# The weight sums of a decoder layer's first output product made ahead, during product pairs two to four

## Chip, cores, metric

The kernel runs on one core of one Trainium2 chip. The metric is the device time of one execution in microseconds (us); lower is better. Everything is float32 at the interface.

## What is computed

One layer of a hybrid decoder on 512 tokens of width 2048. The reference, cut to what matters:

```python
h = rms_norm(x, norm1_g)
proj = h @ w_in                                   # one combined projection
qa, ka, va, ra, ga, qb, kb, vb = split(proj)
out_a = gla_mixer(qa, ka, va, ra, log_g, onorm_g) # 4 heads of gated linear attention
out_b = dilated_mixer(norm(qb), norm(kb), vb)     # 8 heads of dilated attention
mix = concatenate([out_a, out_b])
x = x + mix @ w_out                               # the output product
x = x + (silu(h2 @ w_gate) * (h2 @ w_up)) @ w_down, with h2 = rms_norm(x, norm2_g)
```

The change concerns the left half of `mix @ w_out`: the weight columns 0 to 1023 of `w_out`, a matrix of 2048 x 2048.

## The kernel before

**Products in pairs.** Every large matrix product is done in pairs of weight blocks, two blocks of 512 columns each (`w1`, `w2`), by a scheme of the Strassen-Winograd kind: seven products of half size in place of eight. The object `Pair` (L236) stands for one pair. Its products come in the order P1, P5, P6, P3, P7, P2, P4 (L32), and each runs over `g`, the quarters of its inner dimension (four; three in two of the last pairs). One product at one `g` is called a **group** here; a pair of four quarters is 28 groups.

**The weights of a group.** A quarter of weights is a tile of 128 partitions x 1024 floats, 512 KB, two row blocks (j = 0, 1) of 128 rows x 512 columns. For each `g` there are four quarters, a, b, c, d: a and b are the upper rows of `w1` and `w2`, c and d the lower rows. P1, P3 and P2 use a quarter as it is (a, d, c). P5, P6, P7 and P4 use a difference: b - a, d - a, d - b, c - a, where the minuend of one may be the result of another, since `source` (L250) subtracts in place with one VectorE instruction (L256, 128x1024): P5 leaves b - a in a's tile, and so on. `load_quarter` (L219) loads a quarter through SyncE's DMA queue into the pool `wpool`, which has 12 buffers.

**The split.** Float32 matmuls are made of two rounded parts. `stream` (L318) runs through the groups of all pairs. For each it rounds the weights on ScalarE (`wh`, L331), subtracts that from the weights on VectorE (`wl`, L335, 128x1024), and issues 12 matmuls on TensorE (L372): eight with `wh`, four with `wl`. `wh` and `wl` have two buffers each. The work for group k + 1's parts and group k + 2's sum is written ahead of the matmuls of group k. After the eighth matmul of a group the pair's `step` is called (L378); it carries the background work: attention heads, normalisations, transposes and the building of later operands, so many units for each group (`rate`, `paced`). The operand's side is split in the same manner (ScalarE L174, VectorE L175, 128x512), and its sums are VectorE instructions too (L1256 to L1260 for the late operands).

**What sets the order.** The first pair is laid out by hand. After it, a scheduler orders the instructions of each engine by when it reckons their inputs ready, starting from the program's order; a buffer that is still in use holds its next user.

**The pairs in turn.** The first pair (by hand); va (pair two), query and key of the first four dilated heads (pair three), vb (pair four), the other queries and keys, the gates; then two output pairs (L1438, L1439), eleven pairs of the feed-forward part (FFN) and six of its down projection. In pairs two to four the attention units run in the background. In these, GpSimd does the small steps of `rsqrt_mean` (L158, L159): `so` for an output of a linear-attention head, which VectorE multiplies in at L938, and `ss` for the norms of query and key heads, which VectorE uses at L1086. GpSimd also copies decays (L864, L865) and clears a tile `PT` (L894). It issues no DMAs. The first output pair also builds parts of its own operand while it runs.

**The pool `rpool`** has four buffers of 256 KB: raw input during the first pair, parts of operands later, and one lane of a dilated head.

Of the kernel before, what the change touches and what calls it, by code (L numbers as in the profile page):

```python
# [10 lines left out]
F32 = mybir.dt.float32  # L11
# [3 lines left out]
ALU = mybir.AluOpType  # L15
# [3 lines left out]
P = 128  # L19
# [14 lines left out]
SINGLE = {"P1": "a", "P3": "d", "P2": "c"}  # L34
SUMS_OF = {"P5": "ba", "P6": "da", "P7": "db", "P4": "ca"}
# [72 lines left out]
def block_kernel(ctx: ExitStack, tc: tile.TileContext, ins, out):  # L108
    nc = tc.nc
    x, w_in, w_out, w_gate, w_up, w_down = (  # L110
        ins[n] for n in ("x", "w_in", "w_out", "w_gate", "w_up", "w_down")
    )
# [33 lines left out]
    load = nc.sync.dma_start  # L146
# [18 lines left out]
    class Operand:  # L165


        def __init__(self, groups):
            self.groups = groups
            self.t = {}  # L170
# [65 lines left out]
    class Pair:  # L236


        def __init__(self, op, rows, w1, w2, final, step, scale=None, before=None):
            self.op, self.rows, self.w1, self.w2 = op, rows, w1, w2  # L240
            self.final, self.step, self.scale, self.before = final, step, scale, before
            self.q, self.dst, self.held = {}, {}, {}

        def quarter(self, name, g):
# [5 lines left out]
        def source(self, prod, g):  # L250

            if prod in SINGLE:
                return self.quarter(SINGLE[prod], g)
            one, two = SUMS_OF[prod]
            src = self.quarter(two, g)
            nc.vector.tensor_tensor(src, self.quarter(one, g), src, op=ALU.subtract)  # L256
            return src
# [50 lines left out]
        def end(self, prod):  # L308
            src = self.dst[prod]
            if prod in ("P1", "P5", "P6"):  # L310
                self.held[prod] = self.seeds(src, int(prod == "P5"))
            elif prod == "P4":
                later(1, lambda: self.final(1, 0, None, src), hold=True)
            else:
                which = {"P3": "P6", "P7": "P5", "P2": "P1"}[prod]
                self.close(self.held[which], src, *CLOSES[prod])

    def stream(pairs):  # L318

# [65 lines left out]
    def soon(fn, groups=1):  # L385

        soonest.append([groups, fn])

    def run_soon():
        for d in list(soonest):  # L390
            d[0] -= 1
            if d[0] <= 0:
                soonest.remove(d)
                d[1]()
# [114 lines left out]
    def later(units, fn, hold=False):  # L509

        deferred.append([units, fn, hold])
# [20 lines left out]
    def finish(ready):  # L532

        tries = 0
        while not ready():
            tries += 1
            assert tries < 100
            run_soon()
            try:
                next(background[0])  # L540
            except StopIteration:
                background.pop(0)

    def paced(counts):
        counts = iter(counts)
        return lambda: step(next(counts, 1))

    def rate(*stretches):


        owed = [0.0]
        rates = iter([r for n, r in stretches for _ in range(n)])

        def go():
            owed[0] += next(rates, stretches[-1][1])
            n = owed[0] if owed[0] > 0.3 else 0
            owed[0] = min(owed[0] - (step(n) or 0.0), 1.0)

        return go
# [79 lines left out]
    row_scale = lambda half, m: rs1[:, 2 * half + m : 2 * half + m + 1]  # L639
# [464 lines left out]
    order = (2, 3, 0, 1)  # L1104

    def final_proj(n1, n2):
        def final(half, which, tiles, acc_):
            if tiles is None:
                tiles = emitted(acc_, lambda m: row_scale(half, m))
            name = (n1, n2)[which]  # L1110
            dst = proj[name]
            for m in range(2):
                r = half * 256 + m * P
                put = lambda r=r, m=m: store(dst[r : r + P, :], tiles[m])
                if name[:2] in ("qb", "kb"):
# [183 lines left out]
    opm = Operand(4)  # L1299
    pairs = []  # L1300

    def pair(*args, **kw):
        pairs.append(Pair(*args, **kw))

    pair(opx, rows_in, col(1536), col(1024), final_proj("va1", "va0"), rate((22, 1), (6, 0.6)),
         row_scale, before=lambda: background.extend([gates(), bias_tables()]))
    flow = rate((90, 0.41))
    pair(opx, rows_in, col(3088), col(4112), final_proj("qb0", "kb0"), flow, row_scale)
    pair(opx, rows_in, col(5648), col(5136), final_proj("vb1", "vb0"), flow, row_scale)
    pair(opx, rows_in, col(3600), col(4624), final_proj("qb1", "kb1"), flow, row_scale)  # L1310
    pair(opx, rows_in, col(2048), col(2560), final_gate, rate((5, 0.6), (23, 1.05)), row_scale)


    rows_mix = [(1024 + 256 * g, 256 * order[g]) for g in range(4)]
    x1_d = [dram([P, D], f"x1_d{t}") for t in range(4)]
    xn_d = [dram([P, 2, 512], f"xn_d{b}") for b in range(8)]
    ss2 = const([P, 4, 4], "ss2")
# [33 lines left out]
    def final_out(second):  # L1351
        rest_of = {}

        def ahead(half, which):
            tok = 1 - half
            rest_of[half, which] = residual_loads(
                [2 * tok, 2 * tok + 1], 512 * (2 * second + which),
                lambda t, c: x[t * P : (t + 1) * P, c : c + 512],
            )

        def final(half, which, tiles, acc_):
            tok = 1 - half
            rows = [2 * tok, 2 * tok + 1]
            ch = 2 * second + which
            tiles = residual(tiles, acc_, rest_of.pop((half, which)))
            for m in range(2):
                t = rows[m]
                store(x1_d[t][:, 512 * ch : 512 * ch + 512], tiles[m])
                jk = work("st", (P, DV), bufs=2).bitcast(mybir.dt.bfloat16)
                nc.scalar.activation(  # L1370
                    jk, tiles[m], AF.Square, accum_out=ss2[:, t, ch : ch + 1]
                )
            if second:
                turn = scaled_store(tiles, rows, tok, xn_d[2 * ch : 2 * ch + 2], 4 * ch)

                def rest():
                    turn()
                    if which == 1 and half == 1:
                        background.append(early_jobs(opn, (2, 3), tops, False))
                        background.append(late_jobs(opn, ((2, 3),), tops, bots, False))  # L1380

                later(2, rest)
                if which == 0 and half == 1:
                    output_scales()
            elif which == 0 and half == 1:
                nc.vector.tensor_tensor(part2, ss2[:, :, 0], ss2[:, :, 1], op=ALU.add)
# [35 lines left out]
        turn()  # L1422
        yield

    ocol = lambda c: w_out[:, c : c + 512]
    def output_scales():
        tmp2 = const([P, 4], "tmp2")
        nc.vector.tensor_tensor(tmp2, ss2[:, :, 2], ss2[:, :, 3], op=ALU.add)
# [6 lines left out]
    opn = Operand(4)  # L1435
    tops = [xn_d[2], xn_d[3], xn_d[6], xn_d[7]]
    bots = [xn_d[0], xn_d[1], xn_d[4], xn_d[5]]
    pair(opm, rows_mix, ocol(0), ocol(512), final_out(0), paced([1] * 28))  # L1438
    pair(opm, rows_mix, ocol(1024), ocol(1536), final_out(1), rate((28, 1.2)))  # L1439


# [82 lines left out]
    for j in range(11):  # L1524
        c = slice(512 * j, 512 * j + 512)
# [52 lines left out]
    for i in range(3):  # L1578
        g0 = 4 * i
        rows_d = [(512 * (g0 + g), 512 * (g0 + g) + 256) for g in range(opd[i].groups)]  # L1580
        for np_ in range(2):
            c = 1024 * np_
# [4 lines left out]
                before=(lambda i=i: background.append(down_jobs(i + 1))) if lead else None,  # L1587
# [46 lines left out]
```

## Time and profile before

| what | us |
|---|---|
| median of three runs | 1964.63 |
| lowest, highest | 1964.08, 1965.51 |
| the profiled execution, device time | 1963.27 |
| its span in the trace | 1961.5 |
| product pair two, three, four | 82.9, 87.7, 87.9 |
| first output pair | 83.2 |
| an FFN pair without other work | 74.3 |

The device time of the profiled execution holds 1.8 us around the span. PE is TensorE's matrix unit and PEld its weight loads, which run beside it; DVE is VectorE, ACT ScalarE, POOL GpSimd, SP SyncE, which issues the DMAs. An arrow `x <- y` in a wait means that the first was held until the second ended. L372 is line 372 of the kernel; where a row names tiles, `wl<-wa,wh` is the output and the inputs with their buffer numbers left out. In a row of instruction groups, the numbers behind the bar are the busy time in us, the mean of one in ns, and the idle time of the engine ahead of them. In a row of the timeline they stand in front: start, duration, then engine, line and operation, and in brackets a wait and what ended it. The mean granted TensorE clock of the run was 0.998 of full speed.

### The profile page before, as it was taken

The page shows a single profiled execution, that of the slowest core. Times are in us where ns is not written, and L with a number is a line of the kernel's source. Part 1 is how long each engine was busy: PE and PEld are TensorE (multiplying, and loading weights), DVE is VectorE, ACT ScalarE, POOL GpSimd, SP SyncE. Part 2 cuts the span into 40 slices and gives each one's busy share as a digit, 9 for nine tenths or more (in the row PEclk, how much of TensorE's full clock was granted, in tenths as well). Part 3 has the DMA queues.
Part 4 walks back from the last instruction along what each step waited for, and adds up shares of the span by engine and source line. Part 5 has one row for each costly group of instructions (what it writes and reads, how often), then busy time and mean ns, then how long its engine had stood idle before and what let it go on. Part 6 is the DMA issues. An engine that isn't in the chain of part 4 may idle for free.

```text
span 1961.5 us, 25794 instructions
## 1 busy us (share of the span) xinstructions
PE 1924.8 (98%) x9226; PEld 1670.7 (85%) x9226; DVE 1653.7 (84%) x1851; ACT 1094.3 (56%) x1600; POOL 61.3 (3%) x81
## 2 busy tenths in 40 slices
PE   8999999999999999999999999999999999999999
PEld 6888888888878877888888888888888888888888
DVE  8997787868789889879878878878879989989987
ACT  8564564566766766545545445445546646546443
POOL 0000230010000000000000000000000000000000
PEclk9999999999999999999999999999999999999999
DMA  8457355464666685554553554554555865955761
GB/s 279 137 164 271 107 179 165 134 208 128 215 220 205 214 294 161 173 167 134 178 169 129 177 164 128 177 162 128 177 162 162 299 207 179 317 178 176 248 214 65
DMA packets 237258, 360.45 MB, mean 184 GB/s; under 512 B 18263, under 2 KB 97056, under 8 KB 237129
## 3 DMA queue, kind: packets, MB, share of 16 engines
q1 hardware_dynamic: 236776, 358.59, 57.2%
q8 instruction: 72, 1.18, 0.2%
q14 instruction: 58, 0.47, 0.1%
q10 hardware_dynamic: 352, 0.21, 0.0%
HBM read 296.59 MB, written 64.51 MB: 184 GB/s over the span
## 4 chain that ended last, share of the span: by engine, by line
PE 82%; DVE 8%; DMA 3%; issue 3%; ACT 2%; POOL 1%; SPq 0%; DVEq 0%; ACTq 0%
PE acc L372 74%; PE acc L440 3%; DVE wl L335 3%; DVE wa L256 2%; PE bank L1134 1%; DVE AS L175 1%; PE bank L992 1%; ACT wh L331 1%; DMA xn_d<-oT 1%; PE bank L1024 1%; DMA r<-xn_d 0%; PE bank L777 0%; PE bank L1017 0%; DMA qT<-S_d 0%; DVE AA L175 0%
## 5 line engine op out<-in xcount | busy, mean ns | idle before, releaser
L372 PE MATMUL acc<-wh,AS 128*128 128x512 f32 x3008 | 711.4, 379 | 0.7 <-ACT wh L331 0.6
L372 PEld LDWEIGHTS acc<-wh,AS 128*128 128x128 f32 x3008 | 569.0, 189 | 81.8 <-ACT wh L331 1.9
L331 ACT CAST wh<-wa 128x1024 fp32r<-128x1024 f32 x376 | 394.0, 1048 | 392.3 <-PE acc L372 366.6
L372 PE MATMUL acc<-wh,AA 128*128 128x512 f32 x2256 | 534.8, 380 | 0.0
L335 DVE TENSOR_TENSOR wl<-wa,wh 128x1024 fp32r<-128x1024 f32 x376 | 456.6, 1217 | 70.3 <-ACT wh L331 45.1
L372 PEld LDWEIGHTS acc<-wh,AA 128*128 128x128 f32 x2256 | 427.3, 190 | 61.1 <-ACT wh L331 0.6
L372 PE MATMUL acc<-wl,AS 128*128 128x512 f32 x1504 | 395.4, 385 | 10.4 <-DVE wl L335 10.1
L372 PEld LDWEIGHTS acc<-wl,AS 128*128 128x128 f32 x1504 | 279.5, 189 | 62.5 <-DVE wl L335 21.8
L372 PE MATMUL acc<-wl,AA 128*128 128x512 f32 x1128 | 297.3, 386 | 6.9 <-DVE wl L335 6.7
L372 PEld LDWEIGHTS acc<-wl,AA 128*128 128x128 f32 x1128 | 209.8, 189 | 39.1 <-DVE wl L335 10.1
L331 ACT CAST wh<-wb 128x1024 fp32r<-128x1024 f32 x94 | 98.5, 1049 | 130.1 <-PE acc L372 125.1
L331 ACT CAST wh<-wc 128x1024 fp32r<-128x1024 f32 x94 | 98.4, 1047 | 112.0 <-PE acc L372 104.9
L331 ACT CAST wh<-wd 128x1024 fp32r<-128x1024 f32 x94 | 98.5, 1048 | 105.5 <-PE acc L372 102.0
L256 DVE TENSOR_TENSOR wa<-wc,wa 128x1024 f32<-128x1024 f32 x94 | 114.5, 1222 | 46.0 <-DMA wc<-in_w_gate 24.8
L335 DVE TENSOR_TENSOR wl<-wc,wh 128x1024 fp32r<-128x1024 f32 x94 | 114.7, 1220 | 36.3 <-ACT wh L331 36.1
L335 DVE TENSOR_TENSOR wl<-wd,wh 128x1024 fp32r<-128x1024 f32 x94 | 114.4, 1220 | 35.7 <-ACT wh L331 28.9
L335 DVE TENSOR_TENSOR wl<-wb,wh 128x1024 fp32r<-128x1024 f32 x94 | 113.8, 1217 | 5.7 <-ACT wh L331 5.7
L256 DVE TENSOR_TENSOR wb<-wd,wb 128x1024 f32<-128x1024 f32 x94 | 114.4, 1217 | 1.0 <-DMA wd<-in_w_in 0.5
L256 DVE TENSOR_TENSOR wa<-wb,wa 128x1024 f32<-128x1024 f32 x94 | 113.6, 1219 | 0.8
L256 DVE TENSOR_TENSOR wa<-wd,wa 128x1024 f32<-128x1024 f32 x94 | 112.8, 1216 | 0.1
L298 DVE SCALAR_TENSOR_TENSOR seed<-acc,rs,seed 128x512 f32<-128x512 f32 x96 | 70.5, 745 | 24.6 <-PE acc L372 24.5
L282 ACT ACTIVATE seed<-acc,rs 128x512 f32<-128x512 f32 x96 | 60.6, 681 | 1.4 <-PE acc L372 0.8
(306 smaller groups left out, 1366.6 us busy)
## 6 DMA issues: line engine op xcount, KB each, us to landing
wa<-in_w_gate SPq DMA_DIRECT2D x44, 512.0 KB, 3.8
wb<-in_w_up SPq DMA_DIRECT2D x44, 512.0 KB, 4.1
wd<-in_w_up SPq DMA_DIRECT2D x44, 512.0 KB, 4.3
wc<-in_w_gate SPq DMA_DIRECT2D x44, 512.0 KB, 3.6
wc<-in_w_in SPq DMA_DIRECT2D x28, 512.0 KB, 3.7
wa<-in_w_in SPq DMA_DIRECT2D x24, 512.0 KB, 5.3
wb<-in_w_in SPq DMA_DIRECT2D x24, 512.0 KB, 6.0
wd<-in_w_in SPq DMA_DIRECT2D x24, 512.0 KB, 6.7
```

The costliest lines, as they stand in the source:

```text
L175: nc.vector.tensor_tensor(a[:, :, 1, :], src, a[:, :, 0, :].bitcast(F32), op=ALU.subtract)
L256: nc.vector.tensor_tensor(src, self.quarter(one, g), src, op=ALU.subtract)
L282: nc.scalar.activation(halves(t), unfolded(src[m]), AF.Copy, scale=self.scale(half, m))
L298: nc.vector.scalar_tensor_tensor(halves(seed[m]), unfolded(src[m]), self.scale(half, m), halves(seed[m]), op0=ALU.mult, op1=ALU.add,)
L331: nc.scalar.copy(high[k], sources[k])
L335: nc.vector.tensor_tensor(low[k], sources.pop(k), high[k].bitcast(F32), op=ALU.subtract)
L372: nc.tensor.matmul(p.dst[prod][m], a[:, jj, hl, m * P : (m + 1) * P], folded(w[:, jj, :]), start=fresh and g == 0 and len(terms) == 2 and ...
L440: recent["pe"] = nc.tensor.matmul(dst[prod][m], a[:, jj, hl, m * P : (m + 1) * P], folded(w[:, jj, :]), start=fresh and g == 0 and len(ter ...
L992: nc.tensor.matmul(lp[:, :n], qh[:, b * P : (b + 1) * P], kh[:, :n], start=True, stop=True)
L1024: nc.tensor.matmul(op, vh[:, k, :], lgs[b][:, k * P : (k + 1) * P], start=(k == 0), stop=(k == b))
L1134: nc.tensor.transpose(bk[:, jj, m * P : (m + 1) * P], tiles[m][:, f : f + P], ident)
```

## The change

The 16 sums that the first output pair uses (four products x four `g`) are made during pairs two to four, kept in DRAM, and loaded when they are needed.

- A generator `weight_sums` makes them in eight blocks, one for each `g` and each row block `j`. A block takes 128x512 pieces: a is fetched at its first group, b and d at the next, c at the third, with DMAs on GpSimd's queue into tiles of `rpool`. From the fifth group on it makes one difference a group on VectorE (a = b - a for P5, b = d - b for P7, d = d - a for P6, which is d - b + a as the in-place chain has it, c = c - d for P4), and each is stored one group later, again on GpSimd's queue. The blocks begin at groups 18, 26, ..., 74, counted from the first group of pair two.
- `beside` wraps the `step` of pairs two, three and four, so that the generator advances by one at each group, behind the background work.
- Every instruction of the generator (32 loads of 256 KB, 32 subtractions, 32 stores of 256 KB) is held in program order: it stays behind the instruction traced before it on its engine.
- The first output pair gets `sums`. Its four sum products load a finished sum (512 KB, SyncE's queue, into `wpool`) where `source` subtracted before; a quarter that was used as it is, is forgotten at once. The pair loads 12 quarters and 16 sums in place of 16 quarters.

By the engines' instruction orders of the two kernels, VectorE gets the 32 subtractions and loses 16 of L256; TensorE and ScalarE keep their order but for small swaps in the first output pair, where VectorE's operand splits also move forward; two sums of pairs three and four move back by a few groups on VectorE; GpSimd goes from 86 to 150 instructions; behind the first output pair nothing moves.

```diff
         def source(self, prod, g):
 
             if prod in SINGLE:
-                return self.quarter(SINGLE[prod], g)
+                t = self.quarter(SINGLE[prod], g)
+                if self.sums:
+                    self.q.pop((SINGLE[prod], g))
+                return t
+            if self.sums:
+                t = wpool.tile([P, 2, 512], F32, name=nm("ws"), tag="w")
+                load(t, self.sums[prod, g])
+                return t
             one, two = SUMS_OF[prod]
...
+    def weight_sums(rows, w1, w2, sums):
...
+        def block(start, g, j):
+            t = {}
+
+            def fetch(name):
+                r0 = rows[g][0 if name in "ab" else 1] + P * j
+                t[name] = rpool.tile([P, 512], F32, name=nm("r"), tag="r")
+                pinned(nc.gpsimd.dma_start(t[name], (w1 if name in "ac" else w2)[r0 : r0 + P, :]))
+
+            def less(dst, one, two):
+                pinned(tt(t[dst], t[one], t[two], op=ALU.subtract))
+
+            def put(prod, name):
+                pinned(nc.gpsimd.dma_start(sums[prod, g][:, j, :], t[name]))
+
+            at(start, lambda: fetch("a"))
+            at(start + 1, lambda: fetch("b"))
+            at(start + 1, lambda: fetch("d"))
+            at(start + 2, lambda: fetch("c"))
+            for i, (dst, one, two, prod) in enumerate(
+                (("a", "b", "a", "P5"), ("b", "d", "b", "P7"), ("d", "d", "a", "P6"),
+                 ("c", "c", "d", "P4"))
+            ):
+                at(start + 4 + i, lambda dst=dst, one=one, two=two: less(dst, one, two))
+                at(start + 5 + i, lambda prod=prod, dst=dst: put(prod, dst))
+
+        for i in range(8):
+            block(18 + 8 * i, i // 2, i % 2)
...
+    early_sums = weight_sums(rows_mix, ocol(0), ocol(512), out_sums)
+    pair(opx, rows_in, col(1536), col(1024), final_proj("va1", "va0"),
+         beside(rate((22, 1), (6, 0.6)), early_sums),
...
     flow = rate((90, 0.41))
-    pair(opx, rows_in, col(3088), col(4112), final_proj("qb0", "kb0"), flow, row_scale)
-    pair(opx, rows_in, col(5648), col(5136), final_proj("vb1", "vb0"), flow, row_scale)
+    flowing = beside(flow, early_sums)
+    pair(opx, rows_in, col(3088), col(4112), final_proj("qb0", "kb0"), flowing, row_scale)
+    pair(opx, rows_in, col(5648), col(5136), final_proj("vb1", "vb0"), flowing, row_scale)
...
-    pair(opm, rows_mix, ocol(0), ocol(512), final_out(0), paced([1] * 28))
+    pair(opm, rows_mix, ocol(0), ocol(512), final_out(0), paced([1] * 28), sums=out_sums)
```

More of the change, by code (lines that the diff above doesn't have):

```diff
@@ L236, in block_kernel, with __init__ @@
     class Pair:
-        def __init__(self, op, rows, w1, w2, final, step, scale=None, before=None):
+        def __init__(self, op, rows, w1, w2, final, step, scale=None, before=None, sums=None):
             self.op, self.rows, self.w1, self.w2 = op, rows, w1, w2
             self.final, self.step, self.scale, self.before = final, step, scale, before
+            self.sums = sums
             self.q, self.dst, self.held = {}, {}, {}
@@ L316, in end, with at @@
                 self.close(self.held[which], src, *CLOSES[prod])
+    def weight_sums(rows, w1, w2, sums):
+        tt, pinned = nc.vector.tensor_tensor, tc.keep_in_program_order
+        plan = {}
+        def at(group, fn):
+            plan.setdefault(group, []).append(fn)
+        def block(start, g, j):
[20 more added lines that the diff above has]
+            block(18 + 8 * i, i // 2, i % 2)
+        for n in range(max(plan) + 1):
+            for fn in plan.get(n, ()):
+                fn()
+            yield
     def stream(pairs):
@@ L542, in finish, with beside, both @@
                 background.pop(0)
+    def beside(go, gen):
+        def both():
+            go()
+            next(gen, None)
+        return both
     def paced(counts):
@@ L1303, in pair @@
         pairs.append(Pair(*args, **kw))
-    pair(opx, rows_in, col(1536), col(1024), final_proj("va1", "va0"), rate((22, 1), (6, 0.6)),
+    ocol = lambda c: w_out[:, c : c + 512]
+    rows_mix = [(1024 + 256 * g, 256 * order[g]) for g in range(4)]
+    out_sums = {
+        (prod, g): dram([P, 2, 512], f"{prod}_{g}_d") for prod in SUMS_OF for g in range(4)
+    }
+    early_sums = weight_sums(rows_mix, ocol(0), ocol(512), out_sums)
+    pair(opx, rows_in, col(1536), col(1024), final_proj("va1", "va0"),
+         beside(rate((22, 1), (6, 0.6)), early_sums),
          row_scale, before=lambda: background.extend([gates(), bias_tables()]))
     flow = rate((90, 0.41))
-    pair(opx, rows_in, col(3088), col(4112), final_proj("qb0", "kb0"), flow, row_scale)
-    pair(opx, rows_in, col(5648), col(5136), final_proj("vb1", "vb0"), flow, row_scale)
+    flowing = beside(flow, early_sums)
+    pair(opx, rows_in, col(3088), col(4112), final_proj("qb0", "kb0"), flowing, row_scale)
+    pair(opx, rows_in, col(5648), col(5136), final_proj("vb1", "vb0"), flowing, row_scale)
     pair(opx, rows_in, col(3600), col(4624), final_proj("qb1", "kb1"), flow, row_scale)
     pair(opx, rows_in, col(2048), col(2560), final_gate, rate((5, 0.6), (23, 1.05)), row_scale)
-    rows_mix = [(1024 + 256 * g, 256 * order[g]) for g in range(4)]
     x1_d = [dram([P, D], f"x1_d{t}") for t in range(4)]
@@ L1423, in first_columns @@
         yield
-    ocol = lambda c: w_out[:, c : c + 512]
     def output_scales():
```

## Prediction

> **What bounds the kernel now.** I read the page first: the busy shares and the chain that ended last.
>
> ```profile
> span 1961.5 us, 25794 instructions
> ...
> PE 1924.8 (98%) x9226; PEld 1670.7 (85%) x9226; DVE 1653.7 (84%) x1851; ACT 1094.3 (56%) x1600; POOL 61.3 (3%) x81
> ...
> PE 82%; DVE 8%; DMA 3%; issue 3%; ACT 2%; POOL 1%; SPq 0%; DVEq 0%; ACTq 0%
> ```
>
> PE is the bound, busy for 98% of the span; DVE holds 8% of the chain. So a DVE instruction is worth time only in stretches where PE waits for DVE. The windows view, asked by stage, finds them. Its columns: stretch, length, then busy time with instruction count of PE, PEld, DVE, ACT and POOL, granted clock, DMA share, GB/s. The rows are product pairs two, three and four (where the early work goes); the first output pair whole, then its product P1, its P5 and P6, and the rest (P3 to P4); and, for scale, one undisturbed FFN pair.
>
> ```profile
> 101.30:184.20 82.90, 81.75 (x391) 69.51 (x390) 69.71 (x77) 42.82 (x56) 0.55 (x3) 1.00 0.63 213
> 184.20:271.90 87.70, 87.62 (x438) 75.32 (x437) 69.47 (x83) 48.23 (x103) 23.26 (x26) 1.00 0.57 170
> 271.90:359.80 87.90, 86.42 (x424) 74.88 (x423) 65.57 (x79) 43.64 (x75) 13.01 (x15) 1.00 0.54 168
> 560.80:644.00 83.20, 77.20 (x345) 64.97 (x344) 81.20 (x95) 52.41 (x78) 0.00 (x0) 0.98 0.63 209
> 560.80:577.10 16.30, 13.46 (x58) 10.97 (x57) 15.98 (x21) 11.67 (x19) 0.00 (x0) 0.90 0.68 231
> 577.10:602.60 25.50, 22.34 (x98) 17.68 (x97) 24.86 (x30) 14.87 (x21) 0.00 (x0) 1.00 0.25 81
> 602.60:644.00 41.40, 41.40 (x193) 36.32 (x192) 40.36 (x46) 25.87 (x40) 0.00 (x0) 1.00 0.84 279
> 959.30:1033.60 74.30, 74.30 (x353) 65.09 (x353) 60.19 (x59) 37.12 (x43) 0.00 (x0) 1.00 0.52 160
> ```
>
> A pair is 28 groups. The last stretch of the output pair holds 16 groups, without an idle microsecond on PE: 41.4 / 16 = 2.59 us for a group at full speed. The output pair is 83.2 us, the FFN pair 74.3: some 8.9 us are waste. Of them 25.5 - 8 x 2.59 = 4.8 lie in the eight groups of P5 and P6, where DVE is busy 24.86 of 25.5: there DVE is the bound. The waits of that stretch (total, count, mean) and its DVE groups:
>
> ```profile
> PEld acc L372 <- DVE wl L335: 5.1, 5, 1.6
> PE acc L372 <- DVE wl L335: 3.0, 4, 1.2
> ...
> L256 DVE TENSOR_TENSOR wa<-wd,wa 128x1024 f32<-128x1024 f32 x4 | 4.9, 1220 | 0.0
> ...
> L335 DVE TENSOR_TENSOR wl<-wa,wh 128x1024 fp32r<-128x1024 f32 x7 | 8.5, 1219 | 0.0
> ...
> L175 DVE TENSOR_TENSOR AS<-r,AS 128x512 fp32r<-128x512 f32 x8 | 5.5, 688 | 0.6 <-ACT AS L174 0.6
> ```
>
> Here DVE makes for each group a weight sum (L256, 1.22), a weight's low part (L335, 1.22), and one sum and one split of the operand (L1256 to L1260 and L175, 0.69 each): 3.82 us by the durations, 25.5 / 8 = 3.2 as it ran, because part of it was done ahead. Both are above the 2.59 of PE.
>
> **The change: what it gains in the output pair.** All 16 sums of L256 go from this pair: 16 x 1.22 = 19.5 us of DVE. Twelve or so lie in stretches that PE fills anyway (P7 and P4 wholly: 41.40 busy of 41.40), and give nothing. In P5 and P6 DVE needs 1.22 + 0.69 + 0.69 = 2.60 a group afterwards, just PE's 2.59, so I expect the eight groups at 2.6 to 2.75 instead of 3.2: 3.5 to 4.7 us, taken as 4.2. What is late next is the same wait with a smaller size, since DVE stays full until its backlog is gone in P3.
>
> In P1 the sums of P5 that DVE makes ahead stand in front of work that PE needs:
>
> ```profile
> 568.90 1.13 PE L372 MATMUL acc<-wl,AA 128*128 128x512 f32 x4 [1.03 <-DVE wl L335]
> 569.37 1.22 DVE L256 TENSOR_TENSOR wa<-wb,wa 128x1024 f32<-128x1024 f32 x1
> 571.10 1.29 DVE L1183 TENSOR_TENSOR cr<-cr,og 128x512 f32<-128x512 f32 x2
> 571.85 2.14 PE L1134 MATMUL bank<-mats,cr 128*128 128x128 f32 x8 [1.81 <-DVE cr L1183]
> ```
>
> Without L256 the wait of 1.81 loses up to 1.2. I take 0.8 (0 to 1.5, with some of the clock that fell to 0.90 here). The sum is now loaded: 12 more transfers of 512 KB, 6.3 MB, so 23.7 MB instead of 17.4 (209 x 83.2) in about 79 us, 300 GB/s. The last stretch of this pair moved nearly as much, 279, and P5 and P6 moved 81: there is the room for the new loads. I price them at nothing; if a load came late, a group would wait for it, 1 to 2 us in all. Gain of the pair: **4.2 + 0.8 = 5.0 (3 to 6)**. Behind it the engines' orders are unchanged.
>
> **What it costs in pairs two to four: DVE.** It gets 32 subtractions 128x512. That shape, all in SBUF, costs:
>
> ```profile
> L1488 DVE TENSOR_TENSOR r<-r,r 128x512 f32<-128x512 f32 x11 | 7.5, 681 | 0.0
> ```
>
> 32 x 0.68 = 21.8 us, on an engine that is busy for 69.71, 69.47 and 65.57 us of pairs two to four: 75 to 84%. They hurt only where the low parts (L335) are made just before PE needs them. I compared, group by group, the end of L335 with the matmuls that read it. Two ends of what I found:
>
> ```profile
> 173.21 1.22 DVE L335 TENSOR_TENSOR wl<-wa,wh 128x1024 fp32r<-128x1024 f32 x1
> ...
> 179.03 1.03 PE L372 MATMUL acc<-wl,AA 128*128 128x512 f32 x4
> ...
> 239.00 1.22 DVE L335 TENSOR_TENSOR wl<-wb,wh 128x1024 fp32r<-128x1024 f32 x1
> 240.27 1.13 PE L372 MATMUL acc<-wl,AS 128*128 128x512 f32 x4
> ```
>
> 179.03 - 174.43 = 4.6 us of lead in the first, 240.27 - 240.22 = 0.05 in the second. By the changed kernel's order, five of the eight blocks (the first, third and the last three) subtract at groups whose lead is mostly 2.5 to 5 us; 0.68 a group fits into that and is given back while DVE idles. The other three, at groups 32 to 35, 48 to 50 and 56 to 59 of the stream, stand at or just ahead of groups with leads of 0.05 to 1.5 us (32, 45 to 48, 60 to 64). I count one subtraction paid at each of these three places, 3 x 0.68, **2.0 us**: 0.5 if DVE's idle time behind them catches up, 5 if eight are paid.
>
> **What it costs there: GpSimd.** It gets 64 DMA issues of 256 KB, which no row of before shows on that queue. On SP's queue the same sizes land within (last column, median us from issue):
>
> ```profile
> S_d<-r SPq DMA_DIRECT2D x44, 256.0 KB, 2.0
> r<-p_d SPq DMA_DIRECT2D x44, 256.0 KB, 3.6
> ```
>
> A block subtracts two or three groups (5 to 8 us) behind its loads and stores one group later, so 3.6 is covered. The bytes, 16.8 MB over 258 us, add 65 GB/s to 168 to 213, less than the output pair's 279. What can hurt is the time that an issue holds GpSimd, because its queue runs in order and 12 rsqrt steps of the attention units stand directly behind issues in it, with DVE behind them:
>
> ```profile
> DVE seed L1086 <- POOL ss L159: 6.3, 5, 1.4
> DVE oT L938 <- POOL so L159: 4.6, 7, 1.0
> ```
>
> While DVE waits there, every low part behind L938 or L1086 waits too. The hold's bounds are GpSimd's own shortest and longest of these rows:
>
> ```profile
> 202.77 4.05 POOL L864 COPY decay<-L 128x8 f32<-128x8 f32 x1 [11.13 <-ACT L L859]
> 304.16 0.19 POOL L864 COPY decay<-L 128x8 f32<-128x8 f32 x1 [11.14 <-ACT L L859]
> 187.46 0.52 POOL L894 MEMSET PT<- 128x512 f32 x1 [2.09 <-PE bank L927]
> 234.82 0.52 POOL L894 MEMSET PT<- 128x512 f32 x1 [7.63 <-PE bank L927]
> ```
>
> The copy, which reads SBUF, takes 0.19 or 4.05, which I put down to DVE's work beside it; the memset, which only writes, takes 0.52 both times. An issue writes a list of transfers and reads no tile, so I take the memset's 0.52: 64 x 0.52 = 33 us of GpSimd in 258, one or two of them ahead of a waiting step, under the DVE lead. Cost inside the 2.0 above. At 4.05 it would be the slow rival below.
>
> The Trainium skill (SBUF — State Buffer, Who interferes with whom) says that GpSimd's writing of DMA descriptors is blocked by DVE copies and tensor_scalar operations in their two-port mode, while two-input operations contend with GpSimd's reads; DVE's work here is almost all two-input, and the slow copy beside the steady memset agrees with it, though no row shows a blocked issue. By that rule the issues stay short and the sum stands; where the blocked case held, the time would be that of the slow rival.
>
> **Sum.** Against the profiled execution, 1963.27 us: -5.0 + 2.0 = -3.0, 1960.3. The median of the runs, 1964.63, is 1.4 above it, so I predict 1964.63 - 3.0 = **1961.6**.
>
> **Rivals** (a measurement of this kernel tells about 0.2%, 3.9 us, from no change).
> - *Full gain, free work.* DVE's leads absorb all subtractions and the clock in P1 recovers: -5 to -6.5, about 1959. For it: PE idles only 1.15, 0.08 and 1.48 us in the three pairs. Against: the lead of 0.05 shown above (group 45).
> - *Even.* The early work costs 4 to 6, or the output pair gets only 2 because DVE is still full there, or a sum's load is late: 1963 to 1967, about 1964.6. This holds the case that the change doesn't do what it says: L175 and L335 alone keep DVE at PE's pace.
> - *Slower: an issue holds GpSimd.* The place is the rsqrt steps L158 and L159 behind the issues; two issues use up a lead of 4.6 at 2.3 us each, and the three sites without lead pay from 0.5 us on. At 2 us those three pay for two issues, 12 us, of which I let a third overlap with waits that L158 has already (8): 1961.6 + 8 = 1969.6. At 4.05, all 12 sites pay 2 x 4.05 - 4.6 = 3.5, half of them on PE's path: +21, 1983. For it: the copy's 4.05. Against: the memset's 0.52.
>
> **How the numbers follow.** Forecast (1959.9 to 1963) 0.40, full gain 0.21, even 0.15, slower 0.24. The range runs from 1958.3, low in the full gain, to 1971, in the lower half of the slower case; about 0.06 lies below and 0.12 above. Faster by over 0.2% is the full gain, and the forecast's lowest third: 0.21 + 0.12 = 0.33. Slower by over 0.2% is the slower case with a little of the even one: 0.25. Within: 0.42.
>
> **What would show it.** Right: the output pair lasts 78 to 79 us, its wait of the matmul for L335 in P5 and P6 falls from 5.1 + 3.0 to under 3, and pairs two to four together are 260 to 261 us instead of 258.5. Wrong: waits of DVE for `ss` and `so` above 6.3 and 4.6 by several us or GpSimd busy over 100 us in pairs two to four (an issue holds it); a wait of ACT or DVE for a `ws` load in the output pair; pairs two to four longer by over 5 us with GpSimd idle (DVE or the DMA queues).

## The result, and the profile after

The changed kernel takes 1971.74 us (median of seven runs, 1968.81 to 1974.75); the kernel before, beside it, 1965.16 (1964.08 to 1965.98). The ratio is 1.0033, 95% interval 1.0022 to 1.0045: 6.6 us slower, where 3.0 faster was forecast, and 0.7 above the range's end. The profiled execution of the changed kernel is the slowest of the seven, 1974.75 us, so its trace has some 3 us more than the median has.

The page, of the changed kernel: span, busy shares, and the queue that is new.

```profile
span 1972.7 us, 25957 instructions
...
PE 1934.5 (98%) x9226; PEld 1675.5 (85%) x9226; DVE 1654.9 (84%) x1867; ACT 1094.5 (55%) x1600; POOL 99.6 (5%) x145
...
q0 software_dynamic: 5120, 16.78, 2.4%
```

POOL is 38 us busier. The first block's four loads were issued at 54 to 88 us, before pair two begins: to be held in program order puts an issue behind the instruction before it in GpSimd's own queue, not at a group of TensorE. Pair two begins at 103.5 us here and at 101.3 before; the other runs with early DMAs do not repeat that (100.4 to 101.8). The windows of the same stages as before: pairs two, three and four, then the first output pair, its P1, its P5 and P6, and the rest.

```profile
103.50:186.50 83.00, 81.85 (x392) 69.48 (x391) 71.21 (x80) 42.84 (x56) 3.55 (x8) 1.00 0.65 219
186.50:280.20 93.70, 89.99 (x438) 76.06 (x437) 76.12 (x95) 48.18 (x103) 43.73 (x53) 0.98 0.76 238
280.20:373.00 92.80, 88.35 (x424) 75.81 (x423) 75.51 (x95) 43.42 (x75) 24.72 (x42) 0.98 0.68 226
574.40:656.40 82.00, 77.52 (x345) 66.15 (x344) 65.01 (x79) 52.49 (x78) 0.00 (x0) 0.96 0.90 295
574.40:593.20 18.80, 15.13 (x58) 11.82 (x57) 14.18 (x19) 12.51 (x21) 0.00 (x0) 0.82 0.89 288
593.20:613.90 20.70, 20.70 (x98) 18.12 (x97) 19.86 (x26) 15.99 (x24) 0.00 (x0) 1.00 0.89 294
613.90:656.40 42.50, 41.70 (x193) 36.20 (x192) 30.97 (x35) 23.99 (x34) 0.00 (x0) 1.00 0.90 299
```

Pairs three and four lasted 87.7 and 87.9 us before: they lose 6.0 and 4.9. Of these 10.9 us PE is idle for 6.6 more, and for 4.3 more it is busy with the same number of matmuls: its granted clock there is 0.98, not 1.00. P5 and P6 of the output pair fall from 25.5 to 20.7, eight groups at 2.59, PE without an idle moment: the 4.8 us that DVE cost there are gone. But P1 takes 18.8 instead of 16.3, at a granted clock of 0.82, and the rest 42.5 instead of 41.4.

So the question is what the early work does to pairs three and four. The waits of these two (total, count, longest) after:

```profile
PEld acc L421 <- DVE wl L384: 10.9, 7, 3.8
DVE wa L264 <- DMA wc<-in_w_in: 10.3, 5, 2.8
PE acc L421 <- DVE wl L384: 8.1, 4, 3.4
...
DVE seed L1144 <- POOL ss L159: 5.6, 4, 2.6
...
ACT oT L991 <- DMA ong_d<-oT: 4.7, 1, 4.7
...
DVE oT L996 <- POOL so L159: 3.6, 3, 2.1
```

and before, in their stretch:

```profile
DVE wa L256 <- DMA wc<-in_w_in: 4.9, 5, 1.6
...
PEld acc L372 <- DVE wl L335: 3.1, 4, 1.3
...
ACT oT L933 <- DMA ong_d<-oT: 1.5, 2, 1.1
PE acc L372 <- DVE wl L335: 1.5, 2, 0.9
```

DVE waits no longer for GpSimd than before (5.6 and 3.6 against 6.3 and 4.6). What grew are waits for DMAs: for the c quarters of `w_in`, and for a store of a linear head's output. Such a wait holds an engine's queue, and the low parts behind it come late. The timeline shows the second at its largest (pair four, P5), read from the top:

```profile
294.89 0.92 SPq L999 DMA_DIRECT2D ong_d<-oT  x2
...
300.72 0.38 ACT L991 ACTIVATE oT<-bank 128x256 f32<-128x256 f32 x1 [4.67 <-DMA ong_d<-oT]
...
301.65 0.19 POOL L158 TENSOR_SCALAR so<-so 128x2 f32<-128x2 f32 x1 [5.31 <-ACT oT L991]
...
302.68 0.88 DVE L996 SCALAR_TENSOR_TENSOR oT<-bank,so,gb 128x256 f32<-128x256 f32 x2 [2.12 <-POOL so L159]
...
303.48 1.22 DVE L384 TENSOR_TENSOR wl<-wa,wh 128x1024 fp32r<-128x1024 f32 x1
...
304.75 1.13 PE L421 MATMUL acc<-wl,AS 128*128 128x512 f32 x4 [3.38 <-DVE wl L384]
```

A head's two outputs share one tile `oT`. ScalarE may write the second only when the first has been stored; the store is issued at 294.89 and holds it until 300.72. In the trace of before, ScalarE waited 0.45 there:

```profile
288.12 0.38 ACT L933 ACTIVATE oT<-bank 128x256 f32<-128x256 f32 x1 [0.45 <-DMA ong_d<-oT]
```

A long wait costs PE more than the wait itself. In pair three the c quarters come late, and PE waits 2.56 us; the four matmuls that start 1 us later take 1.76 us, where four of this size take 1.03 without such a wait ahead of them:

```profile
246.89 1.13 PE L421 MATMUL acc<-wl,AS 128*128 128x512 f32 x4 [2.56 <-DVE wl L384]
...
247.86 1.76 PE L421 MATMUL acc<-wh,AS 128*128 128x512 f32 x4
```

The granted clock is 0.50 from 248.0 to 251.4, and again, behind the wait of 3.38, from 306.0 to 309.5; it is 1.00 in the rest of pairs three and four. These two spells of 3.4 us cost 3.4 of the 4.3 us. Before, PE never waited over 0.93 us there, and its clock held at 1.00.

The landing times of the DMAs in pairs three and four (last column, median us) are longer, for the c quarters in single cases more than in the median: 7.3 us at most, against 4.6 before. After:

```profile
P_d<-r POOLq DMA_DIRECT2D x28, 256.0 KB, 3.5
r<-in_w_out POOLq DMA_DIRECT2D x27, 256.0 KB, 4.6
wd<-in_w_in SPq DMA_DIRECT2D x9, 512.0 KB, 8.3
wc<-in_w_in SPq DMA_DIRECT2D x8, 512.0 KB, 4.1
...
wb<-in_w_in SPq DMA_DIRECT2D x8, 512.0 KB, 7.0
ong_d<-oT SPq DMA_DIRECT2D x16, 128.0 KB, 4.9
```

and before:

```profile
wd<-in_w_in SPq DMA_DIRECT2D x9, 512.0 KB, 5.0
wc<-in_w_in SPq DMA_DIRECT2D x8, 512.0 KB, 3.7
...
wb<-in_w_in SPq DMA_DIRECT2D x8, 512.0 KB, 5.1
ong_d<-oT SPq DMA_DIRECT2D x16, 128.0 KB, 2.4
```

**Theory T**, then: the early loads and stores lengthen the landing of transfers that the kernel needs just in time. **Rivals:** D, the 32 subtractions fill VectorE; G, the 64 issues hold GpSimd; N, it is the number of DMAs, not their bytes.

### The profile page after: what moved, and what is told of

Read it like the earlier page. It is cut to its first block, busy times and chain, and to the rows that moved or that the text cites. A ratio compares the mean times of both kernels' runs of the same rounds, so it can differ in the third digit from the quotient of the medians.

```text
span 1972.7 us, 25957 instructions
## 1 busy us (share of the span) xinstructions
PE 1934.5 (98%) x9226; PEld 1675.5 (85%) x9226; DVE 1654.9 (84%) x1867; ACT 1094.5 (55%) x1600; POOL 99.6 (5%) x145
## 4 chain that ended last, share of the span: by engine, by line
PE 60%; DVE 3%; DMA 2%; issue 1%; ACT 1%; SPq 0%; POOL 0%; DVEq 0%; ACTq 0%
PE acc L421 59%; DVE wl L384 1%; PE bank L1192 1%; DMA xn_d<-oT 1%; DVE wa L264 0%; DMA r<-xn_d 0%; ACT wh L380 0%; DMA r<-p_d 0%; DMA p_d<-PT 0%; DVE seed L302 0%; DVE AS L175 0%; DVE seed L1404 0%; DMA q<-in_x 0%; DMA wc<-in_w_out 0%; DVE AA L175 0%
## 5 line engine op out<-in xcount | busy, mean ns | idle before, releaser
L380 ACT CAST wh<-wa 128x1024 fp32r<-128x1024 f32 x364 | 381.5, 1048 | 387.9 <-PE acc L421 357.5
L384 DVE TENSOR_TENSOR wl<-wa,wh 128x1024 fp32r<-128x1024 f32 x364 | 442.4, 1219 | 65.2 <-ACT wh L380 40.4
L380 ACT CAST wh<-wb 128x1024 fp32r<-128x1024 f32 x90 | 94.3, 1049 | 124.8 <-PE acc L421 122.1
L380 ACT CAST wh<-wd 128x1024 fp32r<-128x1024 f32 x94 | 98.4, 1048 | 103.5 <-PE acc L421 99.2
L264 DVE TENSOR_TENSOR wa<-wc,wa 128x1024 f32<-128x1024 f32 x90 | 109.8, 1222 | 50.3 <-DMA wc<-in_w_gate 24.0
L384 DVE TENSOR_TENSOR wl<-wb,wh 128x1024 fp32r<-128x1024 f32 x90 | 108.9, 1218 | 4.7 <-ACT wh L380 4.5
L264 DVE TENSOR_TENSOR wb<-wd,wb 128x1024 f32<-128x1024 f32 x90 | 109.7, 1218 | 3.3 <-DMA wd<-in_w_in 2.8
L264 DVE TENSOR_TENSOR wa<-wb,wa 128x1024 f32<-128x1024 f32 x90 | 108.8, 1220 | 0.8
L264 DVE TENSOR_TENSOR wa<-wd,wa 128x1024 f32<-128x1024 f32 x90 | 108.2, 1217 | 0.1
```

The lines of the kernel that those rows point to most:

```text
L380: nc.scalar.copy(high[k], sources[k])
L384: nc.vector.tensor_tensor(low[k], sources.pop(k), high[k].bitcast(F32), op=ALU.subtract)
```

## The experiments

Each median stands beside that of the kernel before in the same series; the ratio is to it. The runs of the early half or of a part of it also have the output pair's edit of the first one below, so that this pair makes its own sums as before.

| run | median | before | ratio, 95% interval |
|---|---|---|---|
| early half alone | 1976.07 | 1965.21 | 1.0049 (1.0037 to 1.0061) |
| late half alone | 1958.30 | 1965.21 | 0.9959 (0.9947 to 0.9972) |
| early DMAs alone | 1974.72 | 1965.21 | 1.0042 (1.0030 to 1.0054) |
| early subtractions alone | 1964.76 | 1965.21 | 0.9995 (0.9987 to 1.0004) |
| early DMAs, a quarter of the bytes | 1964.71 | 1964.12 | 1.0002 (0.9993 to 1.0010) |
| change, on SyncE's queue | 1962.95 | 1964.12 | 0.9996 (0.9986 to 1.0006) |
| change, second output tile | 1966.86 | 1964.12 | 1.0014 (1.0006 to 1.0023) |
| P5 and P6 only | 1961.33 | 1964.12 | 0.9983 (0.9974 to 0.9992) |
| P5 and P6, second tile | 1957.06 | 1964.22 | 0.9962 (0.9949 to 0.9975) |
| the same, SyncE's queue | 1957.12 | 1964.22 | 0.9962 (0.9948 to 0.9975) |
| early DMAs alone, SyncE's queue | 1969.72 | 1964.22 | 1.0027 (1.0018 to 1.0036) |
| P5 and P6, second tile, spread | 1959.80 | 1964.22 | 0.9977 (0.9968 to 0.9986) |
| second tile alone | 1964.54 | 1964.05 | 0.9998 (0.9989 to 1.0007) |
| early loads alone | 1966.70 | 1964.05 | 1.0012 (1.0003 to 1.0021) |
| early stores alone | 1966.32 | 1964.05 | 1.0013 (1.0003 to 1.0022) |

**The early half alone.**

```diff
-    pair(opm, rows_mix, ocol(0), ocol(512), final_out(0), paced([1] * 28), sums=out_sums)
+    pair(opm, rows_mix, ocol(0), ocol(512), final_out(0), paced([1] * 28))
```

> The early sums are made and stored as in the change, but the output pair makes its own sums again as before (the early ones are not used). Theory T (transfers: the 16.8 MB of early loads and stores lengthen the landing of transfers that the kernel waits for in pairs three and four): pairs three and four lose what they lost in the changed kernel, about 11 us, the output pair is back at 83 us: 8 to 13 us slower than before. Theories D (VectorE is filled by the 32 subtractions) and G (the 64 issues hold GpSimd) expect the same sum; this run only prices the early half by itself. If it is under 5 us slower, the loss lies elsewhere (in the output pair's new loads).

10.9 us slower by the medians. The early half costs what the trace of the change showed, whatever the output pair does with it.

**The late half alone.**

```diff
-        (prod, g): dram([P, 2, 512], f"{prod}_{g}_d") for prod in SUMS_OF for g in range(4)
+        (prod, g): w_out[128 * (4 * i + g) : 128 * (4 * i + g + 1), 0:1024].rearrange(
+            "p (j n) -> p j n", j=2
+        )
+        for i, prod in enumerate(SUMS_OF) for g in range(4)
...
-    early_sums = weight_sums(rows_mix, ocol(0), ocol(512), out_sums)
...
-         beside(rate((22, 1), (6, 0.6)), early_sums),
+         rate((22, 1), (6, 0.6)),
...
-    flowing = beside(flow, early_sums)
+    flowing = flow
```

> No early work. The output pair loads 16 ready tiles of 512 KB (rows of the weight matrix in the shape of the sums, 4 KB in one piece for each partition) where the change loads sums; the differences are left out, so the output is not the reference's. It prices the late half alone. Theory T: P5 and P6 run at 2.59 us a group, 4.8 us gained, and the 6.3 MB of new loads delay parts of the operand in P1 and P3, 2 to 3 us lost: 1.5 to 3 us faster than before. If P1's loss in the changed kernel was the granted clock of that execution alone and not the loads: 4.5 to 6 us faster.

6.9 us faster, more than either case said. The kernel leaves out the differences, so its output is not the reference's. In its trace P5 and P6 take 20.9 us, and P1 16.4 at a full clock. So the new loads do not by themselves bring the loss of P1 that the trace of the change shows.

**The early DMAs alone, and the early subtractions alone.**

```diff
-                at(start + 4 + i, lambda dst=dst, one=one, two=two: less(dst, one, two))
```

> The early half without its 32 subtractions: the 32 loads and 32 stores stay on GpSimd's queue, the output pair works as before; what is stored is the quarters themselves and is not used. Theory T: 6 to 11 us slower than before, with landings of the oT stores near 5 us and of the wc loads later than in the kernel before. Theory D: 0 to 2 us slower. Theory G: 6 to 11 us slower, but then GpSimd's issues or the steps behind them take several us each.

Here `flat` is a constant tile of 128x512:

```diff
-                pinned(nc.gpsimd.dma_start(t[name], (w1 if name in "ac" else w2)[r0 : r0 + P, :]))
...
-                pinned(tt(t[dst], t[one], t[two], op=ALU.subtract))
+                pinned(tt(t[dst], flat, flat, op=ALU.subtract))
...
-                at(start + 5 + i, lambda prod=prod, dst=dst: put(prod, dst))
```

> The early half without its DMAs: 32 subtractions of the same shape at the same places of VectorE's order, on a constant tile, into the same pool; no loads, no stores, the output pair as before; the subtractions' results are not used. Theory T: 0 to 2.5 us slower than before. Theory D: 6 to 11 us slower. Theory G: no change.

DMAs alone: 9.5 us slower. Subtractions alone: no difference (-0.4, the interval holds 1). D falls. The windows of pairs two to four in the run with the subtractions alone show why:

```profile
101.00:183.90 82.90, 81.76 (x391) 69.42 (x390) 71.98 (x81) 42.84 (x55) 0.76 (x3) 1.00 0.63 211
183.90:271.80 87.90, 87.83 (x437) 75.01 (x437) 76.27 (x95) 48.08 (x102) 29.31 (x26) 1.00 0.56 170
271.80:358.90 87.10, 86.23 (x424) 74.89 (x424) 74.50 (x95) 43.73 (x75) 14.34 (x15) 1.00 0.55 171
```

DVE has 18 us more in the three pairs than before, and their lengths (82.9, 87.9, 87.1) are those of before: even where a low part had a lead of 0.05 us, the 0.68 cost nothing that these lengths show. With the DMAs alone, the two kinds of waits that grew in the change are there again:

```profile
ACT oT L990 <- DMA ong_d<-oT: 11.0, 3, 5.2
...
DVE wa L264 <- DMA wc<-in_w_in: 9.7, 5, 4.3
```

**A quarter of the bytes.** As the DMAs alone, with 128 columns of 512 in each.

```diff
-                pinned(nc.gpsimd.dma_start(t[name], (w1 if name in "ac" else w2)[r0 : r0 + P, :]))
+                pinned(nc.gpsimd.dma_start(t[name][:, 0:P], (w1 if name in "ac" else w2)[r0 : r0 + P, 0:P]))
...
-                pinned(nc.gpsimd.dma_start(sums[prod, g][:, j, :], t[name]))
+                pinned(nc.gpsimd.dma_start(sums[prod, g][:, j, 0:P], t[name][:, 0:P]))
```

> As the run with the early DMAs alone (9.5 us slower than before by its median), but each of the 64 DMAs moves 128 of its 512 columns: the same number of DMAs and of row pieces, a quarter of the bytes (4.2 MB); no subtractions, the output pair as before, what is stored is not used. Theory B (bytes in flight delay what the kernel waits for): 0 to 4 us slower than before. Theory N (the number of issues or of row pieces on GpSimd's software queue does it): 7 to 10 us slower.

0.6 us, no difference within the interval. N and G fall: the same number of issues on the same queue costs nothing that can be told from noise. From here on theory T is called B, for bytes. In the trace of the change an issue holds GpSimd for 0.54 us:

```profile
L341 POOL DMA_DIRECT2D r<-in_w_out x32: 538/543/766, 53.7 to 352.9; - x32
```

(shortest, median, longest ns). On this queue it is the bytes, not the issues.

**Loads alone, and stores alone** (the first without the subtractions and stores, the second without loads and subtractions, storing the constant tile `flat`).

```diff
-                at(start + 4 + i, lambda dst=dst, one=one, two=two: less(dst, one, two))
-                at(start + 5 + i, lambda prod=prod, dst=dst: put(prod, dst))
+                pass
```

> Only the 32 early loads (8.4 MB, GpSimd's queue); no subtractions, no stores, nothing of them is used, the output pair as before. Theory B with a loss that grows with the bytes: half of the 9.5 us, 3.5 to 6 us slower than before. If the stores do the harm: 0 to 2 us slower.

```diff
-            at(start, lambda: fetch("a"))
-            at(start + 1, lambda: fetch("b"))
-            at(start + 1, lambda: fetch("d"))
-            at(start + 2, lambda: fetch("c"))
...
-                at(start + 4 + i, lambda dst=dst, one=one, two=two: less(dst, one, two))
...
-                pinned(nc.gpsimd.dma_start(sums[prod, g][:, j, :], t[name]))
+                pinned(nc.gpsimd.dma_start(sums[prod, g][:, j, :], flat))
```

> Only the 32 early stores (8.4 MB, GpSimd's queue), from a constant tile; no loads, no subtractions, nothing of them is used, the output pair as before. Theory B with a loss that grows with the bytes: 3.5 to 6 us slower than before. If the loads do the harm: 0 to 2 us slower.

2.6 and 2.3 us slower, between the two bands that were named for each (0 to 2 and 3.5 to 6). Neither kind does it by itself, and the loss grows faster than the bytes: 4.2 MB cost 0.6, 8.4 MB 2.3 to 2.6, 16.8 MB 9.5. One reason is in the traces: those of the 4.2 and 8.4 MB have no spell of half clock in pairs two to four, while those of the 16.8 MB on GpSimd's queue have one or two, 1.7 us each. That slack takes up the first delays is likely, but was not tried.

**The second output tile.** In the whole change, in the kernel before, and further down:

```diff
-            o = work("oT", (P, 2, DV))
+            o = work("kT" if ts[0] else "oT", (P, 2, DV))
```

> The whole change, and the second output of each linear-attention head gets another tile (that of its spent keys, kT), so that ScalarE's squares no longer wait until the first output's store has landed. If the wait for that store is one of the places where the transfers cost time, 2 to 5 us faster than the changed kernel, about 1968; if it only took the place of another wait: 1970 to 1973.

> The kernel before, with the second tile for the linear heads' outputs and nothing else. In the trace of before, ScalarE waits for the store of the first output for 1.5 us in all: within 1.5 us of before. If it is 3 to 5 us faster, the gain of the runs with the second tile is not a repair of what the early transfers do, but a gain of its own.

In the whole change: 2.7 us slower than before, where the change was 6.6 slower. In the kernel before: no difference. So by the medians the wait for the store is one place of the loss, worth about 4 us. In the trace of the run ScalarE's wait for that store is gone from the list, and the wait for the c quarters stays:

```profile
DVE wa L264 <- DMA wc<-in_w_in: 9.7, 6, 3.2
```

The traces bear out less of it here: pairs three and four take 184.3 us with the tile and 186.5 without, but pair two 84.5 and 83.0, and two spells of half clock remain; the two executions differ most in P1 (15.6 at a clock of 1.00, 18.8 at 0.82). The clear case is further down: with the sums of P5 and P6 only, the tile takes pairs three and four from 180.7 to 175.9 us, against 175.6 before, and the one spell of half clock goes with them.

**SyncE's queue.**

```diff
-                pinned(nc.gpsimd.dma_start(t[name], (w1 if name in "ac" else w2)[r0 : r0 + P, :]))
+                load(t[name], (w1 if name in "ac" else w2)[r0 : r0 + P, :])
...
-                pinned(nc.gpsimd.dma_start(sums[prod, g][:, j, :], t[name]))
+                store(sums[prod, g][:, j, :], t[name])
```

> The whole change with the early loads and stores on SyncE's queue, in the scheduler's order, and only the subtractions held in program order. Theory B: the same bytes at much the same time, so 4 to 9 us slower than before, like the change. Theory N or G (GpSimd's queue is what costs): 1 to 6 us faster than before, which is the output pair's gain less a little.

Like before (ratio 0.9996), so some 8 us faster than with GpSimd's queue, on the side that N and G had claimed. As the quarter of the bytes had ruled these out, a fourth theory was formed, **Q**: on a queue of its own an early transfer shares the DMA engines with whatever SyncE's queue has running, while on one queue the transfers follow each other. In this run's pairs three and four the heads' outputs are stored in 3.0 us, not 4.9:

```profile
ong_d<-oT SPq DMA_DIRECT2D x16, 128.0 KB, 3.0
```

The Trainium skill (DMA: Bandwidth & Descriptors, SWDGE vs HWDGE vs iDMA) says that the DMAs that GpSimd issues and those of SyncE feed different queues inside each DMA engine, which takes turns between them. The 4.9 us beside a second queue and the 3.0 on one agree with it; no run here shows the turns themselves. But Q has a rival that was not tried: the loads were also issued at other times. On GpSimd's queue they stand behind stores that wait for subtractions, and then go out together; from pair two on, 10 of the 27 that follow another load follow it within 0.7 us. On SyncE's queue 1 of 28 does.

The DMAs alone on SyncE's queue, by the same edit without the subtractions, were to settle it:

> The 64 early DMAs alone, as in the run with the early DMAs alone (9.5 us slower than before by the medians), but on SyncE's queue in the scheduler's order; no subtractions, the output pair as before, what is stored is not used. Theory Q: 1 to 6 us slower than before, with oT stores landing in about 3 us instead of 5. Theory B alone: 7 to 11 us slower.

5.5 us slower, against 9.5, in the band of Q; but it does not settle it. Without the subtractions to wait for, 24 of the 32 early loads were issued ahead of pair three, and the loss is another, in pair two:

```profile
PEld bank L685 <- DMA v<-in_onehot: 5.7, 1, 5.7
PE bank L685 <- DMA v<-in_onehot: 5.3, 1, 5.3
```

PE waits there for a load of 66 KB, which it did not wait for in the trace of before, and which stands in the same queue as the early loads. For the whole change a single queue did less harm, to the store's landing and to the time; whether by the order of the transfers or by their times of issue stays open.

**P5 and P6 only**, then with the second tile, then that on SyncE's queue (by the edit above), then that with the blocks spread on GpSimd's queue.

```diff
-                if self.sums:
-                    self.q.pop((SINGLE[prod], g))
+                if self.sums and prod == "P1":
+                    self.q.pop(("a", g))
                 return t
-            if self.sums:
+            if self.sums and prod in ("P5", "P6"):
                 t = wpool.tile([P, 2, 512], F32, name=nm("ws"), tag="w")
                 load(t, self.sums[prod, g])
+                if prod == "P6":
+                    self.q["a", g] = t
                 return t
...
-            at(start + 2, lambda: fetch("c"))
...
-                (("a", "b", "a", "P5"), ("b", "d", "b", "P7"), ("d", "d", "a", "P6"),
-                 ("c", "c", "d", "P4"))
+                (("a", "b", "a", "P5"), ("d", "d", "a", "P6"))
```

> Only the sums of P5 and P6 are made early (16 subtractions, 24 loads, 16 stores: 10.5 MB instead of 16.8); P7 and P4 subtract in the output pair as before. Theory B: the early loss falls to about 10.5/16.8 of 10 us, 6 us, and the output pair keeps its gain of 5 to 7 us: 1964 to 1967. If the early loss goes with single late landings rather than with the amount, 1968 to 1972.

> Only the sums of P5 and P6 early, on GpSimd's queue, and the second tile for the linear heads' outputs. The second tile saved about 4 us in the whole change; with 10.5 MB in flight instead of 16.8 I expect 1 to 3 us from it: 1958.5 to 1960.5, 4 to 6 us faster than before. If the wait moves on to the weight quarters, 1961 as without it.

> The same with the early loads and stores on SyncE's queue. Theory Q (two queues share the DMA engines, so that each transfer that the kernel waits for runs beside an early one; on one queue they follow each other in order): 1 to 4 us faster than on GpSimd's queue, 1956 to 1959. Theory B alone (bytes, whatever the queue): no difference, 1959 to 1961.

```diff
-            block(18 + 8 * i, i // 2, i % 2)
+            block(6 + 10 * i, i // 2, i % 2)
```

> P5 and P6 only, on GpSimd's queue, with the second tile, the blocks ten groups apart from group 6 on instead of eight from group 18. Fewer bytes at a time, but some of them in pair two, which moves more already (213 GB/s). If the density of the early bytes sets the loss, 0.5 to 2 us faster than with the blocks eight apart; if single late landings do, the same within 1 us, or 1 to 3 us slower by new collisions in pair two.

P5 and P6 alone: 2.8 us faster than before, better than expected. With the second tile 7.2 faster, the best of all and better than the 4 to 6 expected, and equal on SyncE's queue (7.1): with the store off the path these runs show no difference between the queues. Spread from group 6 on: 4.4 faster; pair two, which was free, now loses 2.5 us in its trace, so here it seems to have counted more where the bytes fell than how dense they were (the two intervals overlap a little). The windows of the best run (its profiled execution is its fastest, 1954.58 us): the first output pair whole, its P1, its P5 and P6.

```profile
560.20:637.00 76.80, 74.44 (x346) 64.11 (x345) 72.14 (x86) 52.19 (x78) 0.00 (x0) 1.00 0.87 288
560.20:574.80 14.60, 12.24 (x58) 9.64 (x57) 12.23 (x17) 11.71 (x20) 0.00 (x0) 1.00 0.91 299
574.80:595.50 20.70, 20.70 (x97) 18.13 (x96) 20.70 (x28) 17.61 (x27) 0.00 (x0) 1.00 0.86 290
```

P5 and P6 are as short as with all 16 sums, and the eight sums of P7 and P4 stay hidden.

## Why the prediction was wrong

- **The bound, right.** P5 and P6 took 25.1 to 25.5 us in each of the nine traces with L256 in their path, 20.7 to 21.0 in each of the eight without: 4.6 us, forecast 4.2. That the other eight sums give nothing is shown by the run with P5 and P6 only. (The third number in the prediction's rows of waits is the longest wait, not the mean.)
- **P1, mis-sized.** It was put at 0.8. Over all traces P1 takes 16.3 to 19.6 us (mean 18.3 of nine) with L256 and 14.6 to 18.8 (mean 16.4 of eight) without: about 2. The trace of before was the best of its nine, which hid the room. The granted clock of P1 was 1.00 in five of the eight without L256 and 0.80 to 0.91 in all others. Each dip is a spell of 3.4 or 6.8 us at half clock, begun during or shortly after a wait of PE of 1.4 to 2.4 us; but one execution waited 2.1 us in P1 and kept its clock. What decides it was not tried.
- **The late half, mis-sized therefore:** 5.0 forecast, 6.9 measured.
- **The subtractions: 2.0 forecast, none measured.** Leads of 0.05 to 1.5 us at three places were taken as a price. None was paid; the text's lower bound, 0.5 if DVE's idle time catches up, came nearest.
- **The step that failed: the early bytes, priced at nothing.** The prediction asked whether an early load would be in time for its own subtraction (3.6 us "is covered") and whether the mean rate had room (65 GB/s on top of 168 to 213). Both held. It did not ask what the early transfers do to the landing of others, and which of those stand on the path. They cost 9.5 us by themselves. By the waits, that is in two places: the store of `oT` (its landing went from 2.4 to 4.9 us; about 4 us of time by the medians with the second tile) and the weight quarters of `w_in` that come just in time. Where such a wait held PE for over 2.3 us, half clock came on top. Of the signs that the prediction had named for being wrong, the last one came: pairs two to four took 269.5 us instead of 258.5, without longer waits for GpSimd.
- **The slower rival: right sign, wrong mechanism.** An issue holds GpSimd for 0.54 us, as the forecast's own estimate of 0.52 had it, and DVE's waits for `so` and `ss` did not grow. The Trainium skill (SBUF — State Buffer, Who interferes with whom) says that `tensor_tensor`, DVE's two-input operation, did not stall such DMAs as its copies did, and these 0.54 us agree.
- **The sum.** Early half +10.9 and late half -6.9 make +4.0; the change measured +6.6 with runs from +3.7 to +9.6. Two things lie in this gap: P1's clock of 0.82, and in P3 0.2 to 1.1 us more where all 16 sums are loaded, none where eight are. Neither was taken apart further.

## What to carry to other kernels

Before moving bytes into a stretch with a mean rate to spare, list which transfers of that stretch are waited for, loads just in time and stores that free a single-buffered tile alike, and take their landing as longer: here the doubling of a 128 KB store's 2.4 us cost more than all 32 instructions that came with the bytes. Look for waits of PE that grow past some 2 us, since half clock may follow them. Move only the part of the work whose removal shortens a bound stretch (eight sums of 16 here), and give the tile behind a slow store a second buffer first.

## What the runs showed of the hardware

A DMA issue on GpSimd's queue holds that engine for 0.54 us in the median, 0.77 at most, and a 256 KB load lands 4.6 us later. Stretches at 0.54 to 0.57 of DMA share are not free for more: on that queue 8.4 MB over these and pair two (0.63) cost 2.3 to 2.6 us, twice that 9.5. In pairs two to four of all 17 traces, PE's waits of 2.3 to 5.3 us, six of them, were each followed by a granted clock of 0.50 for 3.4 or 6.8 us; of the four between 1.9 and 2.3 three were, and of the shorter ones none. And the mean granted clock of one stretch, P1, was 1.00 or 0.80 to 0.91 from run to run.
